# RWKV's gram matrices and state outputs: matmuls over 64 rows, two heads in turn, without zeros between them

## The chip, the cores and the metric

The kernel runs on one core of one Trainium2 chip. The time is the device time of one execution in microseconds (us), the median over runs. In the profile PE is TensorE's matmul, PEld its weight load, DVE VectorE, ACT ScalarE, POOL GpSimd, SP SyncE.

## The reference

One residual block of a decoder over 512 tokens of width 2048: an RWKV-7 time mixing and a sliding-window attention run in parallel, are merged by gates, and a gated ConvFFN follows. The change is inside the time mixing. Its recurrence has 16 heads of 64 channels:

```
def step(state, inp):
    r_t, k_t, v_t, w_t, ka_t, kb_t = inp        # ka = -kk, kb = kk * a
    sa = jnp.einsum('bhvk,bhk->bhv', state, ka_t)
    state = (state * w_t[:, :, None, :] + sa[..., None] * kb_t[:, :, None, :]
             + v_t[..., None] * k_t[:, :, None, :])
    y = jnp.einsum('bhvk,bhk->bhv', state, r_t)
    return state, y
_, y = lax.scan(step, state0, xs)
```

## The kernel before

The sequence is cut into 8 chunks (NCH) of 64 tokens (C), and the 16 heads into 8 pairs. A pair lies on the 128 partitions (rows): head 0 of the pair on rows 0 to 63, head 1 on rows 64 to 127 (`HV`). `early(p)` projects and prepares the inputs of pair p, `late(p, st)` does the recurrence by chunks, `final(p, st)` normalises and gates the result. Between the pairs `emit_gate` projects gate columns that are needed later. All projections go through `project` (L258 to L260), three float32r matmuls per weight tile into an accumulator `acc`; their weights are split into two parts by ACT (`whi`, L243) and DVE (`wlo`, L244).

In `late`, for every chunk n and head h:

- BKK holds the decayed kb and k of a head side by side as stationary operand (128 rows, 128 columns), BAR the decayed -kk and r as moving operand. The gram matmul (L645) gives all four products of a chunk for each head. Since both heads lie in the 128 rows of one matmul, BAR has a place for each head (`[P, NCH, 2, 2, C]`), in which the other head's rows are zero: 256 moving columns per chunk, half of them zeros in either half of the rows. Two chunks go to one PSUM bank of the pool `bulk`, which has three; DVE masks the bank into AB (L648) and MM (L649).
- AB is inverted in steps (X, AI, BT, BX; L650 to L710), with transposes through PE (L661, L671, L675, L707).
- The chain over the chunks: psG = AB and the state SV (L714), psU = BX and G (L718), psS = KK and UV (L725), and DVE makes the next state SV (L727).
- The output of a chunk: UV and MM (L735), to which the state SV and r of BAR are added (L737) in the same place of PSUM. Both have 128 rows and 64 stationary columns; SV has zeros in the rows of the other head's part of BAR or is met there by zeros.

All these are plain float32 matmuls, and one shows as two records on PE. The tiles and their dependencies are handled by a framework that also sets the order of each engine's instructions: unless the code pins it, it puts the program's instructions into an order of its own for each engine, so that projection matmuls stand between the steps of the chain.

Of the kernel before, what the change touches and what calls it, by code (L numbers as in the profile page):

```python
# [8 lines left out]
F32 = mybir.dt.float32  # L9
# [4 lines left out]
ALU = mybir.AluOpType  # L14
# [4 lines left out]
P = 128  # L19
# [3 lines left out]
C = 64  # L23
NCH = S // C
# [110 lines left out]
def block_kernel(ctx: ExitStack, tc: tile.TileContext, d: Dims, a: dict, out: bass.AP):  # L135
    nc = tc.nc
    act, dve, pool, pe, sync = nc.scalar, nc.vector, nc.gpsimd, nc.tensor, nc.sync
# [42 lines left out]
    def col(nm, i=0):  # L180
        return pcol[:, PR[nm] + i : PR[nm] + i + 1]
# [23 lines left out]
    def split(hi, lo, src, pin=free):  # L205
        pin(act.activation(hi, src, AF.Copy))
        pin(dve.tensor_tensor(lo, src, hi.bitcast(F32) if hi.dtype == F32R else hi, op=ALU.subtract))
# [75 lines left out]
    if True:  # L283
# [3 lines left out]
        with tc.tile_pool(name="x0_ps", bufs=6, space=PSUM) as ps0:  # L287
# [10 lines left out]
            for h in range(2):  # L298
                hs = slice(h * HT * P, (h + 1) * HT * P)
                for k in range(NK):  # L300
                    ps = ps0.tile([P, HT * P], F32, name="ps_x", tag="x")
                    for t in range(HT):
                        pe.transpose(ps[:, t * P : (t + 1) * P], xt[h * HT + t][:, k * P : (k + 1) * P], ident)
                    g = col("n1g", k)
# [43 lines left out]
        with ExitStack() as pt:  # L348
# [4 lines left out]
            def small():  # L353
                return mps.tile([P, S], F32, name="mi", tag="mi")
# [26 lines left out]
            for t in range(NKV):  # L381
# [12 lines left out]
                ps = small().rearrange("p (n c) -> p n c", c=P)  # L394
                for b in range(NT):
                    pe.transpose(ps[:, b], vf[:, b * P : (b + 1) * P], ident)
                ps = ps.rearrange("p n (h c) -> p n h c", c=HD)
# [16 lines left out]
            for g in range(NHK):  # L414
# [7 lines left out]
                for n in range(NT):  # L422
# [4 lines left out]
                    for j in range(GQ // 2):  # L427
                        for e in range(2):
                            hs = slice(e * HD, (e + 1) * HD)
# [4 lines left out]
                    for h in range(GQ):  # L434
                        slope = float(2.0 ** (-8.0 * (g * GQ + h + 1) / d.HQ))
                        dve.scalar_tensor_tensor(sc[:, h, k0:], K["dist"][:, k0:], slope, scp[h % 2][:, h // 2, k0:],
                                                 op0=ALU.mult, op1=ALU.add)
# [17 lines left out]
                    for kb in kbs:  # L455
                        ps = small().rearrange("p (h c) -> p h c", c=P)
# [3 lines left out]
                    ps = small()  # L460
                    for kb in kbs:
                        for i, (v, p) in enumerate(((0, 0), (0, 1), (1, 0))):
                            pe.matmul(ps, vhl[v][:, n - 1 + kb, g].rearrange("p e c -> p (e c)"),  # L463
                                      phl[p][:, kb].rearrange("p h c -> p (h c)"),
                                      start=kb == kbs[0] and i == 0, stop=kb == kbs[-1] and i == 2)
                    ps = ps.rearrange("p (h c) -> p h c", c=P)
# [6 lines left out]
        with ExitStack() as pr:  # L473
            lp = pr.enter_context(tc.tile_pool(name="lora", bufs=1, reuse_waits="tile"))
            zp_ = pr.enter_context(tc.tile_pool(name="zpad", bufs=1, reuse_waits="tile"))
            bd = pr.enter_context(tc.tile_pool(name="bd", bufs=1, reuse_waits="tile"))
# [15 lines left out]
            def wtile(tag, bufs=1):  # L492
                return wk.tile([P, S], F32, name=tag, tag=tag, bufs=bufs)

            def bulk():
                return blk.tile([P, S], F32, name="bulk", tag="bulk")
# [15 lines left out]
            for i in range(NG):  # L512
                acc = ztile(d.c_gd + i * P)
                t = wtile("lw")
# [11 lines left out]
            BV = bd.tile([P, NCH, P], F32, name="BV")  # L526
            pool.memset(BV, 0.0)
            BKK = bd.tile([P, NCH, P], F32, name="BKK")
            BAR = bd.tile([P, NCH, 2, 2, C], F32, name="BAR")
            pool.memset(BAR[0:C, :, 1], 0.0)  # L530
            pool.memset(BAR[C:P, :, 0], 0.0)
            AB, MM, KK, SV, UV = (bd.tile([P, NCH, 2, C], F32, name=n) for n in ("AB", "MM", "KK", "SV", "UV"))
            pool.memset(SV[0:C, 0, 0], 0.0)
            pool.memset(SV[C:P, 0, 1], 0.0)
# [4 lines left out]
            def r3(ap, c=C):  # L539
                return ap.rearrange("p (n c) -> p n c", c=c)  # L540

            HV = ((0, C), (C, P))
# [72 lines left out]
            def late(p, st):  # L615
                ag, Ei, kk, kb, k2, rz, vz, bon = st
                Eex, Ein = Et[:, :, 0:C], Et[:, :, 1:]
                kb3, k23, Ei3, kk3, rz3, vz3 = (r3(x) for x in (kb, k2, Ei, kk, rz, vz))
                for h, (lo, hi) in enumerate(HV):
                    ol, oh = HV[1 - h]  # L620
                    hs = slice(lo, hi)
                    dve.tensor_tensor(BKK[hs, :, lo:hi], kb3[hs], Ei3[hs], op=ALU.mult)
                    dve.tensor_tensor(BKK[hs, :, ol:oh], k23[hs], Ei3[hs], op=ALU.mult)
                    dve.scalar_tensor_tensor(BAR[hs, :, h, 0], kk3[hs], -1.0, Eex[hs], op0=ALU.mult, op1=ALU.mult)
                    dve.tensor_tensor(BAR[hs, :, h, 1], rz3[hs], Ein[hs], op=ALU.mult)
                    act.activation(BV[hs, :, ol:oh], vz3[hs], AF.Copy)
                ee = wk.tile([P, NCH], F32, name="ee", tag="ee")
                act.activation(ee, Et[:, :, C], AF.Copy)

# [4 lines left out]
                HN = NCH // 2  # L634

                def mb(nm, n, h=None):
                    m = K[nm] if h is None else K[nm][h[0] : h[1]]
                    return m.unsqueeze(1).to_broadcast([m.shape[0], n, m.shape[-1]])

                BKE = wk.tile([P, NCH, P], F32, name="BKE", tag="BKE")  # L640
                dve.tensor_tensor(BKE, BKK, ee.unsqueeze(2).to_broadcast([P, NCH, P]), op=ALU.mult)
                for n0 in range(0, NCH, 2):
                    ps = bulk().rearrange("p (q c) -> p q c", c=P)
                    for j in range(2):
                        pe.matmul(ps[:, 2 * j : 2 * j + 2].rearrange("p q c -> p (q c)"), BKK[:, n0 + j],  # L645
                                  BAR[:, n0 + j].rearrange("p h a c -> p (h a c)"), start=True, stop=True)
                    q2 = lambda t: t[:, n0 : n0 + 2].rearrange("p n h c -> p (n h) c")
                    dve.tensor_tensor(q2(AB), ps[:, :, 0:C], mb("strict", 4), op=ALU.mult)  # L648
                    dve.tensor_tensor(q2(MM), ps[:, :, C:P], mb("incl", 4), op=ALU.mult)  # L649
                for g in range(2):  # L650
                    ns = slice(g * HN, (g + 1) * HN)
                    for h, (lo, hi) in enumerate(HV):
                        own = AB[lo:hi, ns, h]
                        (dve.tensor_copy if h else act.copy)(BX[lo:hi, ns, lo:hi], own)
                        dve.tensor_tensor(tt[lo:hi, ns], own, mb("m1", HN, (lo, hi)), op=ALU.mult)
                        act.copy(own, BAR[lo:hi, ns, h, 0])
                    dve.tensor_tensor(tt[:, ns], tt[:, ns], mb("istack", HN), op=ALU.add)
                    split(X[:, 0, ns], X[:, 1, ns], tt[:, ns])
                    ps = bulk().rearrange("p (n c) -> p n c", c=P)
                    for j in range(HN):  # L660
                        pe.transpose(ps[:, j], BX[:, g * HN + j], ident)  # L661
                    at_ = wk.tile([P, HN, P], F32, name="at_", tag="at_")
                    dve.scalar_tensor_tensor(at_, ps, SG, mb("idsg", HN), op0=ALU.mult, op1=ALU.add)
                    split(AI[:, 0, ns], AI[:, 1, ns], at_)
                    for i in range(2):
                        dve.tensor_tensor(BT[:, i, ns], AI[:, i, ns], mb("t1bd", HN), op=ALU.mult)
                for g in range(2):
                    ns = slice(g * HN, (g + 1) * HN)
                    ps = bulk().rearrange("p (n c) -> p n c", c=P)
# [3 lines left out]
                    ps = bulk().rearrange("p (n h c) -> p n h c", h=2, c=C)  # L673
# [14 lines left out]
                for m in LEVELS[1:]:  # L688
                    last = m == LEVELS[-1]
                    ps = bulk()  # L690
# [4 lines left out]
                    ps = bulk()  # L695
# [4 lines left out]
                    if not last:  # L700
                        act.activation(X[:, 0], r3(ps), AF.Copy, scale=sc)
                        dve.scalar_tensor_tensor(X[:, 1], r3(ps), sc, X[:, 0], op0=ALU.mult, op1=ALU.subtract)
                        for g in range(2):
                            ns = slice(g * HN, (g + 1) * HN)
                            ps = bulk().rearrange("p (n c) -> p n c", c=P)
# [5 lines left out]
                for n in range(NCH):  # L711
                    ps = chn.tile([P, C], F32, name="psG", tag="chn")
# [4 lines left out]
                    ps = chn.tile([P, C], F32, name="psU", tag="chn")  # L717
# [5 lines left out]
                    ps = chn.tile([P, C], F32, name="psS", tag="chn")  # L723
                    for h, (lo, hi) in enumerate(HV):
                        pe.matmul(ps[lo:hi], KK[:, n, h], UV[:, n, h], start=True, stop=True)  # L725
                    for h, (lo, hi) in enumerate(HV):
                        dve.scalar_tensor_tensor(SV[lo:hi, n + 1, h], SV[lo:hi, n, h], ee[lo:hi, n : n + 1], ps[lo:hi],  # L727
                                                 op0=ALU.mult, op1=ALU.add)


                ps = bulk()
                for n in range(NCH):
                    for h, (lo, hi) in enumerate(HV):
                        dst = r3(ps)[lo:hi, n]
                        pe.matmul(dst, UV[:, n, h], MM[:, n, h], start=True, stop=n == 0)  # L735
                        if n:
                            pe.matmul(dst, SV[:, n, h], BAR[:, n, h, 1], start=False, stop=True)  # L737
                yhl = wk.tile([P, 2, S], F32R, name="yhl", tag="rhl")
                split(yhl[:, 0], yhl[:, 1], ps)
                return ag, bon, yhl  # L740
# [23 lines left out]
            for p in range(NP):  # L764
                lt = late(p, st)
                if p + 1 < NP:
                    st = early(p + 1)
                final(p, lt)
                for _ in range(GATES_PER_PAIR * NK // 16):
                    emit_gate()  # L770
# [72 lines left out]
    with ExitStack() as pbb:  # L843
# [8 lines left out]
        g = {}  # L852
        for m, i in order:
            hi, lo, r0, n, gi = parts[i]
# [11 lines left out]
            if second:  # L866
                w = min(XC, d.D)
                for e in range(m * XC, (m + 1) * XC, w):
                    t, c0 = divmod(e, d.D)
# [475 lines left out]
def build(nc, arrays, d):  # L1345
    aps = {
        k: nc.dram_tensor(f"in_{k}_dram", v.shape, mybir.dt.from_np(v.dtype), kind="ExternalInput").ap()
        for k, v in arrays.items()
    }
    out = nc.dram_tensor("out_0_dram", (S, d.D), F32, kind="ExternalOutput").ap()  # L1350
    with tile.TileContext(nc) as tc:
        block_kernel(tc, d, aps, out)
# [11 lines left out]
```

## Time and profile before

| | |
|---|---|
| median of 3 runs | 2932.01 us (2930.34 to 2932.07) |
| the profiled execution | 2934.35 us, span 2932.5 us |
| granted TensorE clock | 0.997 |
| the eight pairs, 330 to 1190 us of the span | PE 856 us busy of 860 |
| gram matmuls L645 | 64, two records each |
| output matmuls L735, L737 | 128 and 112, two records each |

In the timeline a row is a run of equal instructions: the start in us from the span's start, the length in us, engine, line, operation, the tile written and the tiles read, then for PE the shape of the stationary operand as rows*columns and of the moving one as rows x elements, and the count. A bracket behind it is idle time before it and what ended that. The ends of matmuls are modelled and successive matmuls overlap, so the distance between starts says how long one occupies PE.

### The profile page before, as it was taken

Reading aid. Unit: us, or ns where it says so; the run is one execution under the profiler, and the core shown is the slowest. Engines: PE = TensorE matmul, PEld = TensorE weight load, DVE = VectorE, ACT = ScalarE, POOL = GpSimd, SP = SyncE. Lnnn points to the kernel's source line nnn. Section 1 sums busy time; section 2 is a strip of 40 time slices with the busy share of each in tenths; the row PEclk is TensorE's granted clock in tenths of the full one; section 3 lists DMA queues with packets and bytes.
Section 4 is the critical chain, followed back from the end, with each engine's and each line's share of the span. In section 5 each row is a group of like instructions: output and inputs, shape, how many; then the busy total and the mean of one; then the engine's idle time right before and its main releaser. Section 6 shows DMA issues by size and latency. Waiting matters only on the chain.

```text
span 2932.5 us, 47976 instructions
## 1 busy us (share of the span) xinstructions
PE 2885.5 (98%) x18654; PEld 2457.4 (84%) x18654; DVE 1978.9 (67%) x3279; ACT 1322.7 (45%) x2147; POOL 219.3 (7%) x286
## 2 busy tenths in 40 slices
PE   7999999999999999999999899999999999999999
PEld 5777777777777777788888899999999999888887
DVE  4577666766766766445567877777777777665555
ACT  4345434434434434332356455455555554544444
POOL 0001000000000000101000001101111011000000
PEclk9999999999999999999999999999999999999999
DMA  7855755656655655877877789888888888877775
GB/s 212 221 151 160 184 136 147 167 137 150 166 137 151 165 134 149 264 226 231 294 248 237 191 232 240 237 226 225 230 238 241 233 226 231 313 240 244 255 258 188
DMA packets 225140, 609.44 MB, mean 208 GB/s; under 512 B 24768, under 2 KB 44944, under 8 KB 223888
## 3 DMA queue, kind: packets, MB, share of 16 engines
q1 hardware_dynamic: 157504, 434.92, 45.1%
q0 software_dynamic: 36064, 132.14, 23.5%
q10 hardware_dynamic: 31344, 39.31, 3.9%
q8 instruction: 146, 2.39, 0.3%
q14 instruction: 82, 0.67, 0.1%
HBM read 556.62 MB, written 174.43 MB: 249 GB/s over the span
## 4 chain that ended last, share of the span: by engine, by line
PE 92%; DMA 3%; DVE 2%; ACT 2%; issue 1%; ACTq 0%; SPq 0%; POOL 0%; DVEq 0%; POOLq 0%
PE X L1065 17%; PE acc L260 11%; PE acc L259 11%; PE acc L258 10%; PE X L932 10%; PE Y L932 8%; PE Y L1065 8%; PE Z L1065 4%; PE bulk L645 1%; PE bulk L707 1%; PE psG L714 1%; PE psS L725 1%; PE mi L463 1%; PE scp L430 1%; PE bulk L553 1%; PE bulk L684 1%
## 5 line engine op out<-in xcount | busy, mean ns | idle before, releaser
L260 PE MATMUL acc<-xhi,wlo 128*128 128x512 f32 x1152 | 471.4, 409 | 0.0
L258 PE MATMUL acc<-xhi,whi 128*128 128x512 f32 x1152 | 465.4, 404 | 3.2 <-DVE xlo L306 1.9
L259 PE MATMUL acc<-xlo,whi 128*128 128x512 f32 x1152 | 465.3, 404 | 0.0
L243 ACT ACTIVATE whi<-raw 128x512 fp32r<-128x512 f32 x352 | 220.1, 629 | 440.9 <-PE acc L259 345.8
L925 DVE TENSOR_TENSOR wlo<-raw,whi 128x1024 fp32r<-128x1024 f32 x210 | 257.1, 1225 | 206.1 <-ACT whi L924 206.0
L244 DVE TENSOR_TENSOR wlo<-raw,whi 128x512 fp32r<-128x512 f32 x352 | 240.5, 689 | 213.0 <-ACT whi L243 206.7
L924 ACT ACTIVATE whi<-raw 128x1024 fp32r<-128x1024 f32 x210 | 222.6, 1060 | 289.3 <-PE X L932 150.9
L1065 PE MATMUL X<-b,whi 128*128 128x256 f32 x1472 | 270.6, 284 | 2.3 <-DVE u L1085 0.9
L1065 PE MATMUL X<-t,whi 128*128 128x256 f32 x1408 | 260.0, 285 | 10.0 <-DVE u L1085 9.5
L1048 DVE TENSOR_TENSOR wlo<-raw,whi 128x1024 fp32r<-128x1024 f32 x176 | 215.1, 1223 | 78.3 <-ACT whi L1047 78.1
L1065 PE MATMUL Y<-t,whi 128*128 128x256 f32 x1408 | 257.1, 283 | 0.0
L258 PEld LDWEIGHTS acc<-xhi,whi 128*128 128x128 f32 x1152 | 217.5, 189 | 44.0 <-issue 3.2
L260 PEld LDWEIGHTS acc<-xhi,wlo 128*128 128x128 f32 x1152 | 217.1, 189 | 43.5 <-issue 2.5
L259 PEld LDWEIGHTS acc<-xlo,whi 128*128 128x128 f32 x1152 | 217.4, 189 | 42.6 <-issue 2.7
L1047 ACT ACTIVATE whi<-a 128x1024 fp32r<-128x1024 f32 x132 | 139.3, 1056 | 215.2 <-DVE a L1041 213.8
L1065 PEld LDWEIGHTS X<-b,whi 128*128 128x128 f32 x1472 | 230.8, 193 | 3.1 <-issue 2.4
L1065 PEld LDWEIGHTS X<-t,whi 128*128 128x128 f32 x1408 | 221.9, 194 | 10.6 <-DVE u L1085 6.9
L1065 PEld LDWEIGHTS Y<-t,whi 128*128 128x128 f32 x1408 | 219.6, 192 | 0.0
L1065 PE MATMUL X<-b,wlo 128*128 128x256 f32 x736 | 209.2, 284 | 2.1 <-DVE wlo L1048 2.1
L1048 DVE TENSOR_TENSOR wlo<-a,whi 128x1024 fp32r<-128x1024 f32 x132 | 161.7, 1226 | 67.3 <-ACT whi L1047 66.7
L1065 PE MATMUL X<-t,wlo 128*128 128x256 f32 x704 | 200.4, 285 | 0.0
L1065 PE MATMUL Y<-t,wlo 128*128 128x256 f32 x704 | 199.2, 283 | 0.0
(343 smaller groups left out, 6073.1 us busy)
## 6 DMA issues: line engine op xcount, KB each, us to landing
raw<-in_w_up_dram SPq DMA_DIRECT2D x180, 512.0 KB
raw<-in_w_z_dram SPq DMA_DIRECT2D x288, 256.0 KB
s_dn<-in_w_dn_dram POOLq DMA_DIRECT2D x88, 512.0 KB, 6.5
raw<-in_w_up_dram POOLq DMA_DIRECT2D x88, 512.0 KB, 8.4
raw<-s_dn SPq DMA_DIRECT2D x88, 512.0 KB
raw<-in_w_dn_dram SPq DMA_DIRECT2D x66, 512.0 KB
a<-in_w_up_dram SPq DMA_DIRECT2D x48, 512.0 KB
s_dn<-in_w_dn_dram SPq DMA_DIRECT2D x44, 512.0 KB
```

The source lines that it names most:

```text
L243: act.activation(hi, raw, AF.Copy)
L244: dve.tensor_tensor(lo, raw, hi.bitcast(F32), op=ALU.subtract)
L258: pe.matmul(acc, whi[:, j], xhi[:, k], start=first, stop=False)
L259: pe.matmul(acc, whi[:, j], xlo[:, k], start=False, stop=False)
L260: pe.matmul(acc, wlo[:, j], xhi[:, k], start=False, stop=last)
L430: pe.matmul(scp[e][:, j, k0:], qn[j][hs, ts], kd[g][hs, n * P - BLK + k0 : (n + 1) * P], start=True, stop=True)
L924: act.activation(whi, wr, AF.Copy)
L925: dve.tensor_tensor(wlo, wr, whi.bitcast(F32), op=ALU.subtract)
L932: pe.matmul(dst, l[:, q, ts], r[:, es], start=fst and j == 0, stop=lst and j == 2, skip_group_check=True)
L1047: pin(act.activation(hi, t, AF.Copy))
L1048: pin(dve.tensor_tensor(lo, t, hi.bitcast(F32), op=ALU.subtract))
L1065: pin(pe.matmul(ps, l[:, k], r[:, k], start=start and k + i == 0, stop=last and i == 2, skip_group_check=True))
```

## The change

BAR loses the zeros: it is `[P, NCH, 2, C]`, with -kk and r of both heads each in its own half of the rows. The DVE writes of BAR run over 128 partitions, two per pair instead of four. The gram matmuls become two per chunk, one over rows 0 to 63 and one over rows 64 to 127, with 128 moving columns each; the two heads go into two banks, four chunks per bank. The masks then work by head on four chunks instead of by two chunks of both heads. The second output matmul (L738 now) takes only the head's 64 rows of SV and BAR.

```
-            BAR = bd.tile([P, NCH, 2, 2, C], F32, name="BAR")
-            pool.memset(BAR[0:C, :, 1], 0.0)
-            pool.memset(BAR[C:P, :, 0], 0.0)
+            BAR = bd.tile([P, NCH, 2, C], F32, name="BAR")
...
-                    dve.scalar_tensor_tensor(BAR[hs, :, h, 0], kk3[hs], -1.0, Eex[hs], op0=ALU.mult, op1=ALU.mult)
-                    dve.tensor_tensor(BAR[hs, :, h, 1], rz3[hs], Ein[hs], op=ALU.mult)
                     act.activation(BV[hs, :, ol:oh], vz3[hs], AF.Copy)
+                dve.scalar_tensor_tensor(BAR[:, :, 0], kk3, -1.0, Eex, op0=ALU.mult, op1=ALU.mult)
+                dve.tensor_tensor(BAR[:, :, 1], rz3, Ein, op=ALU.mult)
...
-                for n0 in range(0, NCH, 2):
-                    ps = bulk().rearrange("p (q c) -> p q c", c=P)
-                    for j in range(2):
-                        pe.matmul(ps[:, 2 * j : 2 * j + 2].rearrange("p q c -> p (q c)"), BKK[:, n0 + j],
-                                  BAR[:, n0 + j].rearrange("p h a c -> p (h a c)"), start=True, stop=True)
-                    q2 = lambda t: t[:, n0 : n0 + 2].rearrange("p n h c -> p (n h) c")
-                    dve.tensor_tensor(q2(AB), ps[:, :, 0:C], mb("strict", 4), op=ALU.mult)
-                    dve.tensor_tensor(q2(MM), ps[:, :, C:P], mb("incl", 4), op=ALU.mult)
+                for g in range(2):
+                    ns = slice(g * HN, (g + 1) * HN)
+
+                    pss = [bulk().rearrange("p (q c) -> p q c", c=P) for _ in HV]
+                    for j in range(HN):
+                        for ps, (lo, hi) in zip(pss, HV):
+                            n = g * HN + j
+                            pe.matmul(ps[:, j], BKK[lo:hi, n], BAR[lo:hi, n].rearrange("p a c -> p (a c)"), start=True, stop=True)
+                    for h, ps in enumerate(pss):
+                        dve.tensor_tensor(AB[:, ns, h], ps[:, :, 0:C], mb("strict", HN), op=ALU.mult)
+                        dve.tensor_tensor(MM[:, ns, h], ps[:, :, C:P], mb("incl", HN), op=ALU.mult)
...
-                        act.copy(own, BAR[lo:hi, ns, h, 0])
+                        act.copy(own, BAR[lo:hi, ns, 0])
...
-                            pe.matmul(dst, SV[:, n, h], BAR[:, n, h, 1], start=False, stop=True)
+                            pe.matmul(dst, SV[lo:hi, n, h], BAR[lo:hi, n, 1], start=False, stop=True)
```

The framework orders the engines anew. On PE, at the gram of the second pair (pair 1), the rows stood like this before (line, operation, tile written and tiles read, size of the output, count):

```order
L260 MATMUL acc<-xhi,wlo 128x512
L645 MATMUL bulk<-BAR,BKK 128x256 x8
L258 MATMUL acc<-xhi,whi 128x512
L259 MATMUL acc<-xlo,whi 128x512
L260 MATMUL acc<-xhi,wlo 128x512
L258 MATMUL acc<-xhi,whi 128x512
L259 MATMUL acc<-xlo,whi 128x512
L260 MATMUL acc<-xhi,wlo 128x512
L661 MATMUL bulk<-ident,BX 128x128 x4
```

Six projection matmuls stood between the gram and the first transposes of BX. On PE at the same place after the change:

```order
L260 MATMUL acc<-xhi,wlo 128x512
L647 MATMUL bulk<-BAR,BKK 128x128 x16
L258 MATMUL acc<-xhi,whi 128x512
L259 MATMUL acc<-xlo,whi 128x512
L260 MATMUL acc<-xhi,wlo 128x512
L258 MATMUL acc<-xhi,whi 128x512
L259 MATMUL acc<-xlo,whi 128x512
L260 MATMUL acc<-xhi,wlo 128x512
L258 MATMUL acc<-xhi,whi 128x512
L259 MATMUL acc<-xlo,whi 128x512
L260 MATMUL acc<-xhi,wlo 128x512
L662 MATMUL bulk<-ident,BX 128x128 x4
```

Nine stand there now, and the eight gram matmuls are sixteen. Within the sixteen, with the numbers of the banks (4431 and 4445 are head 0's two banks, 4432 and 4446 head 1's) and with what an instruction waits for, the rows on PE from the fourth chunk on are:

```order
L647 MATMUL bulk_4431<-BAR_2919,BKK_2918 128x128
L647 MATMUL bulk_4432<-BAR_2919,BKK_2918 128x128
L647 MATMUL bulk_4445<-BAR_2919,BKK_2918 128x128 x4
L647 MATMUL bulk_4446<-BAR_2919,BKK_2918 128x128 [waits DVE_49,PE_49]
L647 MATMUL bulk_4446<-BAR_2919,BKK_2918 128x128 x3
L258 MATMUL acc_5016<-xhi_187,whi_5019 128x512 [waits Activation_49]
```

The first four chunks go head by head in turn; of the last four, head 0's stand together, and then head 1's, the first of which waits for DVE. The other pairs but pair 0 have the same order.

On PE, at two steps of the chain in the output of a chunk, before (psS belongs to the chain, the bulk rows are the output):

```order
L336 MATMUL bulk<-ident,rq_5096 8x128
L725 MATMUL psS<-UV,KK 64x64
L735 MATMUL bulk<-MM,UV 64x64
L737 MATMUL bulk<-BAR,SV 64x64
L725 MATMUL psS<-UV,KK 64x64
L735 MATMUL bulk<-MM,UV 64x64
L737 MATMUL bulk<-BAR,SV 64x64
L577 MATMUL bulk<-wl,thw 128x128 x2
```

And the same place on PE after the change, where lines have moved by one or two:

```order
L336 MATMUL bulk<-ident,rq_5106 8x128
L575 MATMUL bulk<-wl,thw 128x128
L726 MATMUL psS<-UV,KK 64x64
L736 MATMUL bulk<-MM,UV 64x64
L738 MATMUL bulk<-BAR,SV 64x64
L575 MATMUL bulk<-wl,thw 128x128
L726 MATMUL psS<-UV,KK 64x64
L736 MATMUL bulk<-MM,UV 64x64
L738 MATMUL bulk<-BAR,SV 64x64
L575 MATMUL bulk<-wl,thw 128x128 x2
```

The output matmuls keep their places behind the chain's; a projection-like matmul has moved in between the two heads. In the whole program L738 stands 112 times directly behind L736 or L726, both of 128 rows and 64 columns; behind it stands a matmul of 128 columns 94 times and one of 128 rows and 64 columns 18 times.

## The prediction

> **What bounds the kernel now.** I read the page first: busy time and the chain that ended last.
>
> ```profile
> span 2932.5 us, 47976 instructions
> PE 2885.5 (98%) x18654; PEld 2457.4 (84%) x18654; DVE 1978.9 (67%) x3279; ACT 1322.7 (45%) x2147; POOL 219.3 (7%) x286
> PE 92%; DMA 3%; DVE 2%; ACT 2%; issue 1%; ACTq 0%; SPq 0%; POOL 0%; DVEq 0%; POOLq 0%
> ```
>
> TensorE is busy 98% of the span and carries 92% of the last chain. Next came the table by stages, for the stretch in which the eight pairs of heads are worked on:
>
> ```profile
> 330.00:1190.00 860.00, 856.01 (x6143) 645.68 (x6142) 572.94 (x1255) 351.31 (x708) 53.77 (x68) 1.00 0.58 149
> ```
>
> PE is busy 856.01 of 860 us there, at full clock, and DVE 572.94. Between the small matmuls of a pair stand projection matmuls (acc), so nearly every wait of the chain is already filled. What the change adds to PE lengthens the kernel one to one, and what it takes from DVE or POOL is worth nothing unless PE waits for it. The answer for the tile BAR lists what the change touches:
>
> ```profile
> L737 PE MATMUL bulk<-BAR,SV x224: 222/222/222, 391.6 to 1183.9; 128*64 128x64 f32 x112
> L645 PE MATMUL bulk<-BAR,BKK x128: 377/379/483, 335.7 to 1111.9; 128*128 128x256 f32 x128
> L625 DVE TENSOR_TENSOR BAR<-rz,Et x16: 676/687/691, 331.3 to 1086.4; 64x512 f32<-64x512 f32 x16
> ```
>
> One f32 matmul is two records on PE: 64 gram matmuls give 128, 112 output matmuls 224. The durations (222, 379 ns) overlap, so I price by the distance from start to start, in the timeline.
>
> **The output matmuls.** These are consecutive rows of PE's timeline (start, length, line, shape, count), one step of the chain in pair 0:
>
> ```profile
> 390.73 0.40 PE L259 MATMUL acc<-xlo,whi 128*128 128x512 f32 x1
> 390.96 0.40 PE L260 MATMUL acc<-xhi,wlo 128*128 128x512 f32 x1
> 391.29 0.33 PE L725 MATMUL psS<-UV,KK 128*64 128x64 f32 x2
> 391.45 0.28 PE L735 MATMUL bulk<-MM,UV 128*64 128x64 f32 x2
> 391.57 0.28 PE L737 MATMUL bulk<-BAR,SV 128*64 128x64 f32 x2
> 391.78 0.50 PE L258 MATMUL acc<-xhi,whi 128*128 128x512 f32 x1
> 392.12 0.40 PE L259 MATMUL acc<-xlo,whi 128*128 128x512 f32 x1
> ```
>
> A projection matmul takes 0.23 us (390.73 to 390.96), a pair of 128x64 records 0.12 us (391.45 to 391.57). Where the stationary tile changes shape, from 128*128 to 128*64, there is more: 390.96 to 391.29 is 0.33, so 0.10 over, and the pair behind it takes 0.16 instead of 0.12. I read this as PE emptying the array (0.10) and then loading weights with nothing running over the load (0.04). Going back: L737 to L258 is 0.21, 0.09 over, and L258 to L259 is 0.34, 0.11 over.
>
> After the change the second output matmul uses 64 rows: its shape is 64*64, while the one ahead of it (L735, now L736) stays 128*64. L737 had its neighbour's shape and cost 0.12; L738 is a third shape. In the new order all 112 L738 stand directly behind a 128*64 matmul. Behind them come 94 times a 128*128 matmul (a change of shape there before as well, at the same price) and 18 times another 128*64 one, a further new change. That makes 130 new changes. Streaming itself gets no shorter: 64 moving columns either way.
>
> The trace has no change from 128*64 to 64*64. Nearest is one where rows alone change, 128*128 to 64*128, in the attention scores (L430), which work on 64 rows with the two heads in turn:
>
> ```profile
> 191.68 0.39 PE L259 MATMUL acc<-xlo,whi 128*128 128x512 f32 x1
> 192.00 0.49 PE L430 MATMUL scp<-kd,qn 64*128 64x128 f32 x4
> 192.42 0.50 PE L260 MATMUL acc<-xhi,wlo 128*128 128x512 f32 x1
> 192.76 0.39 PE L258 MATMUL acc<-xhi,whi 128*128 128x512 f32 x1
> ...
> 131.39 0.39 PE L260 MATMUL acc<-xhi,wlo 128*128 128x512 f32 x1
> 131.71 0.72 PE L430 MATMUL scp<-kd,qn 64*128 64x128 f32 x8
> 132.35 0.50 PE L258 MATMUL acc<-xhi,whi 128*128 128x512 f32 x1
> 132.69 0.39 PE L259 MATMUL acc<-xlo,whi 128*128 128x512 f32 x1
> ```
>
> 191.68 to 192.00 is 0.32, again 0.09 over. Columns alone (L260 to L725) and rows alone cost the same, so I take the cost of entering a 64-column shape, 0.10 + 0.04 = 0.14 us: 130 x 0.14 = 18.2 us, all on PE and uncovered. The ends: nothing (0), if rows may change freely between shapes of 64 columns; 0.09 + 0.11 = 0.20 as for 128 columns, 130 x 0.20 = 26 us. A gain is excluded, since no streaming is saved.
>
> The Trainium skill (TensorEngine Tiling (Array Packing), Key Properties) says that changing the tiling mode, unlike moving between tiles of one mode, drains TensorE, with no figure; by it the sum keeps the 18.2 and the end of 0 falls away. No run here shows it yet for these two shapes.
>
> **The gram matrices.** Before, eight matmuls stand in a row in pair 1:
>
> ```profile
> 446.98 0.39 PE L260 MATMUL acc<-xhi,wlo 128*128 128x512 f32 x1
> 447.21 3.62 PE L645 MATMUL bulk<-BAR,BKK 128*128 128x256 f32 x16
> 450.47 0.58 PE L258 MATMUL acc<-xhi,whi 128*128 128x512 f32 x1
> 450.89 0.39 PE L259 MATMUL acc<-xlo,whi 128*128 128x512 f32 x1
> ```
>
> From 447.21 to 450.89, less one projection slot of 0.23, is 3.45 us. After, they are 16 matmuls of shape 64*128 moving 128 columns, exactly L430's shape at 192.00 and 131.71. With 4 records (two in each half of the rows) the block lasts 0.42 to the next start, with 8 (four in each) 0.64: so 0.11 per record of one half, the other half running beside it at no cost. Around it stand 0.10 on entry and 0.11 on the matmul behind. A block with m records in the longer half costs 0.10 + 0.42 + 0.11 (m - 2) + 0.11. Fully alternating, m = 16: 2.17 us, a gain of 1.28.
>
> The order on PE does not alternate fully. It has the first eight in turn (8 records in each half), then four of head 0 in a row, then four of head 1 behind a wait for DVE; those last two stretches run one behind the other. So m = 8 + 8 + 8 = 24: 0.63 + 22 x 0.11 = 3.05 us. The wait is for head 0's first bank, which two mask products must have read:
>
> ```profile
> 447.84 0.69 DVE L244 TENSOR_TENSOR wlo<-raw,whi 128x512 fp32r<-128x512 f32 x1 [2.02 <-ACT whi L243]
> 448.45 0.42 DVE L648 TENSOR_TENSOR AB<-bulk,cst 128x256 f32<-128x256 f32 x1
> 448.79 0.41 DVE L649 TENSOR_TENSOR MM<-bulk,cst 128x256 f32<-128x256 f32 x1
> 449.13 0.42 DVE L648 TENSOR_TENSOR AB<-bulk,cst 128x256 f32<-128x256 f32 x1
> ```
>
> DVE is free at 448.45; the first eight end at about 447.21 + 0.10 + 0.21 + 7 x 0.11 = 448.29. A record lasts some 0.17 beyond its slot (L645: 379 ns against 0.21 from start to start), so I let head 0's masks begin at 448.55 and end near 449.3 (0.34 to the second, which lasts 0.41). PE reaches head 1 at 448.29 + 0.88 = 449.17 and waits 0.15. The gain is 3.45 - 3.05 - 0.15 = 0.25 us, 7 x 0.25 = 1.8 us.
>
> Pair 0 is ordered otherwise. There PE waited for DVE before:
>
> ```profile
> 335.74 1.89 PE L645 MATMUL bulk<-BAR,BKK 128*128 128x256 f32 x8
> 337.28 0.58 PE L258 MATMUL acc<-xhi,whi 128*128 128x512 f32 x1
> 337.70 0.40 PE L259 MATMUL acc<-xlo,whi 128*128 128x512 f32 x1
> 339.20 1.99 PE L645 MATMUL bulk<-BAR,BKK 128*128 128x256 f32 x8 [1.10 <-DVE bon L612]
> 340.84 0.58 PE L260 MATMUL acc<-xhi,wlo 128*128 128x512 f32 x1
> ```
>
> DVE now writes BAR in two operations over 128 partitions instead of four over 64 (687 ns each), so it is about 1.4 us earlier, and the 1.10 goes: 1.1 us gained. I count nothing for the rest of that gram, which is split in two blocks with waits of its own. In the other pairs PE doesn't wait for the writes of BAR, and the same saving is worth nothing. The masks keep count and size; BKK, the copies and the transposes stay; two POOL memsets at 274 us go, off the path. The transposes of BX stand nine projection matmuls behind the gram instead of six, 9 x 0.23 = 2.1 us, about what the masks that now end last need.
>
> **Sum.** 18.2 - 1.8 - 1.1 = +15.3 us. The profiled execution took 2934.35 us around a span of 2932.5 and becomes 2949.7; the median of the runs, 2932.01, lies 2.3 lower and becomes **2947 us**, 0.5% slower.
>
> **Rivals.** (a) *The change of rows is free* while the columns stay 64: then only the 2.9 us gained at the gram remain, 2929, not slower. For it: the row halves share columns. Against it: 0.09 us at 192.00, where only rows change. It decides for no loss once a change of shape costs under 2.9/130 = 0.02 us. (b) *Half the price:* the emptying is paid on entering 64*64 alone and no load is laid bare, 112 x 0.10 = 11.2, less 2.9, is +8.3: 2940. (c) *The gram overlaps fully*, m = 16: 7 x 1.28, and in pair 0 two blocks of m = 8 (1.29 each) for two of 1.73 (335.74 to 337.70 less 0.23), 0.9; 9.8 gained and 18.2 - 9.8 = +8.4: 2940. The rows of L430 show the overlap, the written order speaks against it. The Trainium skill (TensorE: Matmul & The Clock Gate, Part 3) has matmuls in distinct row groups run concurrently, which is what L430 shows and what (c) would need throughout. (d) *Dearer:* masks that come behind one more wlo (L244, 0.6 us up to the next start) in seven pairs, 4 us: 2951; or 0.20 per change, 26 - 2.9 = +23: 2955.
>
> **How the numbers follow.** The forecast with its own range 2942 to 2951 gets 0.62; (a) 0.08, (b) 0.10, (c) 0.05, (d) 0.12, and 0.03 for (a) and (c) together, 2922. The range 2938 to 2955 holds the forecast, (b), (c) and (d). A measurement can tell about 0.2%, 5.9 us: slower 0.88 (forecast, b, c, d), same 0.08 (a), faster 0.04.
>
> **What would show it.** In PE's timeline after: L736 to L738 about 0.21 to 0.22 apart instead of 0.12 (right), or still 0.12 (rival a). The L738 pair to a projection matmul 0.25 instead of 0.21, as its own first load is bare. The gram of pair 1 from its first start to the matmul behind it about 3.1 us long, with a short wait for DVE MM (L650) before head 1's last four. A pair some 2 us longer (130/8 x 0.14 less 0.25). I am wrong if the 18 changes back, or the drains, run beside other work, or if PE waits for BX longer than it did.

## The result, and the profile after

| | median us | lowest to highest | runs |
|---|---|---|---|
| before | 2932.01 | 2930.34 to 2935.64 | 5 |
| after | 2947.66 | 2941.75 to 2952.69 | 5 |

The ratio is 1.0052, with a 95% interval of 1.0040 to 1.0063: the changed kernel is 0.5% slower. 2947 us, and 2938 to 2955, were predicted. The profiled execution of after is its longest run: 2952.69 us around a span of 2950.9, at a mean granted clock of 0.997.

The page of after, span, busy time and the chain that ended last:

```profile
span 2950.9 us, 48234 instructions
PE 2903.3 (98%) x18782; PEld 2464.2 (84%) x18782; DVE 1973.5 (67%) x3263; ACT 1323.1 (45%) x2147; POOL 216.8 (7%) x284
PE 93%; DMA 2%; DVE 2%; ACT 1%; issue 1%; ACTq 0%; DVEq 0%; POOLq 0%; SPq 0%
```

PE has 17.8 us more of busy time than before (2903.3 against 2885.5), and the span 18.4 us more. DVE has 5.4 us less and POOL 2.5, and neither shows in the time. The same stretch of the pairs as before, in the table by stages:

```profile
330.00:1190.00 860.00, 857.33 (x6176) 641.79 (x6174) 560.78 (x1218) 348.06 (x698) 52.78 (x67) 1.00 0.60 146
```

PE is as full as it was (857.33 of 860 us, at full clock), so PE doesn't wait more than it did: it takes longer for the same work. How much longer is read from the start of a pair's gram to the start of the next one's. PE's timeline of before has at the last pair (pair 7):

```profile
1108.45 0.39 PE L260 MATMUL acc<-xhi,wlo 128*128 128x512 f32 x1
1108.68 0.59 PE L645 MATMUL bulk<-BAR,BKK 128*128 128x256 f32 x2
```

and that of after has there:

```profile
1121.59 0.39 PE L260 MATMUL acc<-xhi,wlo 128*128 128x512 f32 x1
1121.91 0.60 PE L647 MATMUL bulk<-BAR,BKK 64*128 64x128 f32 x6
```

Pair 1 starts at 447.21 before and at 448.55 after (below). Six periods are 661.47 us before and 673.36 after, so one is 110.25 and 112.23 us: **+1.98 us for each pair**. This period is the measure that the experiments go by. It moved much less than the time in the one repetition there is: in a second profiled execution of after it was 112.28, while the spans were 2950.9 and 2946.7.

The output of a chunk in PE's timeline of after, at the place that the prediction shows of before:

```profile
390.79 0.50 PE L258 MATMUL acc<-xhi,whi 128*128 128x512 f32 x1
391.12 0.40 PE L259 MATMUL acc<-xlo,whi 128*128 128x512 f32 x1
391.45 0.33 PE L726 MATMUL psS<-UV,KK 128*64 128x64 f32 x2
391.61 0.28 PE L736 MATMUL bulk<-MM,UV 128*64 128x64 f32 x2
391.82 0.33 PE L738 MATMUL bulk<-BAR,SV 64*64 64x64 f32 x2
392.08 0.50 PE L260 MATMUL acc<-xhi,wlo 128*128 128x512 f32 x1
```

L736 to L738 is 0.21 us (0.12 before), and L738 to the projection matmul 0.26 (0.21 before): 0.09 + 0.05 = 0.14 us for entering the shape 64*64. The records themselves got longer by this too, not shorter for their half of the rows; the answer for the tile BAR says so for all 224 (222 ns before):

```profile
L738 PE MATMUL bulk<-BAR,SV x224: 218/242/267, 390.5 to 1200.9; 64*64 64x64 f32 x112
```

The gram of pair 1, on PE:

```profile
448.24 0.39 PE L260 MATMUL acc<-xhi,wlo 128*128 128x512 f32 x1
448.55 3.22 PE L647 MATMUL bulk<-BAR,BKK 64*128 64x128 f32 x32
451.70 0.50 PE L258 MATMUL acc<-xhi,whi 128*128 128x512 f32 x1
452.04 0.40 PE L259 MATMUL acc<-xlo,whi 128*128 128x512 f32 x1
```

From 448.24 to 452.04, less two slots of 0.23, is 3.34 us, against 3.45 before. The masks on DVE at that time:

```profile
449.10 0.69 DVE L244 TENSOR_TENSOR wlo<-raw,whi 128x512 fp32r<-128x512 f32 x1 [2.02 <-ACT whi L243]
449.75 0.42 DVE L649 TENSOR_TENSOR AB<-bulk,cst 128x256 f32<-128x256 f32 x1
450.09 0.41 DVE L650 TENSOR_TENSOR MM<-bulk,cst 128x256 f32<-128x256 f32 x1
```

And two rows of the answer for the tile BAR, on what its readers and writers waited for, and who waited for them (us in all, times):

```profile
its engine sat idle before it (us, times) until:
...
  PE bulk L647: 1.5, 7
who waited for it (us, times):
...
  PEld bulk L647: 1.5, 7
```

PE's weight load (PEld) sits idle once in each of seven pairs, 1.5 us in all, 0.21 each, ahead of head 1's last four. The order printed above the prediction lists two waits there, for DVE and for PE itself (`[waits DVE_49,PE_49]`). Head 0's MM ends on DVE at 450.50, and the load starts at 450.62. The profile names PE's own gram matmul as what ended the wait, not the masks. The two came so close together that the run can't tell them apart; if the profile names the right one, earlier masks alone would have gained nothing.

Last, PE's waits in the pairs 1 to 7. Before, first a row of the list of waits (total, times, longest), then its instance in pair 1 in the timeline:

```profile
PE bulk L684 <- ACT AI L206: 1.5, 6, 0.3
```

```profile
459.07 0.20 PE L684 MATMUL bulk<-XIW,AI 128*128 128x64 f16 x1 [0.26 <-ACT AI L206]
```

After, the same list has only this:

```profile
PE bulk L336 <- DVE rq L197: 0.4, 1, 0.4
```

A pair has two AI tiles, one for each half of its chunks, and the triangular inverse begins with matmuls on them. Before, the first matmul on the second AI waited 0.25 us in each pair for ACT to write it. After, it stands here:

```profile
460.57 0.40 PE L258 MATMUL acc<-xhi,whi 128*128 128x512 f32 x1
460.81 0.20 PE L685 MATMUL bulk<-XIW,AI 128*128 128x64 f16 x1
```

In the new order 22 projection matmuls stand between the gram and it instead of 19, two of them directly ahead of it, and the wait is gone. The prediction has no term for it.

### The profile page after: what moved, and what is told of

Same layout as the page of the kernel before. It is cut to its first block, busy times and chain, and to the rows that moved or that the text cites. A ratio compares the mean times of both kernels' runs of the same rounds, so it can differ in the third digit from the quotient of the medians.

```text
span 2950.9 us, 48234 instructions
## 1 busy us (share of the span) xinstructions
PE 2903.3 (98%) x18782; PEld 2464.2 (84%) x18782; DVE 1973.5 (67%) x3263; ACT 1323.1 (45%) x2147; POOL 216.8 (7%) x284
## 3 DMA queue, kind: packets, MB, share of 16 engines
q8 instruction: 147, 2.41, 0.3%
## 4 chain that ended last, share of the span: by engine, by line
PE 93%; DMA 2%; DVE 2%; ACT 1%; issue 1%; ACTq 0%; DVEq 0%; POOLq 0%; SPq 0%
PE X L1066 17%; PE acc L260 11%; PE acc L259 11%; PE acc L258 11%; PE X L933 10%; PE Y L933 8%; PE Y L1066 8%; PE Z L1066 4%; PE bulk L738 1%; PE bulk L708 1%; PE psS L726 1%; PE psG L715 1%; PE bulk L647 1%; PE mi L463 1%; PE scp L430 1%; PE bulk L685 1%
## 5 line engine op out<-in xcount | busy, mean ns | idle before, releaser
L258 PE MATMUL acc<-xhi,whi 128*128 128x512 f32 x1152 | 463.6, 402 | 4.7 <-ACT whi L243 2.8
L1049 DVE TENSOR_TENSOR wlo<-raw,whi 128x1024 fp32r<-128x1024 f32 x176 | 214.9, 1222 | 77.8 <-ACT whi L1048 77.8
L258 PEld LDWEIGHTS acc<-xhi,whi 128*128 128x128 f32 x1152 | 217.3, 189 | 48.0 <-ACT whi L243 4.0
```

The costliest lines, as they stand in the source:

```text
L258: pe.matmul(acc, whi[:, j], xhi[:, k], start=first, stop=False)
L1049: pin(dve.tensor_tensor(lo, t, hi.bitcast(F32), op=ALU.subtract))
```

## The experiments

Theory A is the prediction's: the loss is PE's price for each change of shape in the order in which its matmuls are issued, 0.14 us into 64 columns, so it follows the number of changes and not the number of 64-row matmuls. The rivals put the loss elsewhere: in the gram and the order that comes with it, or in the 64-row output matmul itself, wherever it stands. The texts ahead of each run use letters for them and give each one's numbers. Each run is compared with the kernel before on the same chip.

**The outputs alone.** The kernel before, with its zeros, gram and masks, and only the second output matmul on 64 rows:

```
-pe.matmul(dst, SV[:, n, h], BAR[:, n, h, 1], start=False, stop=True)
+pe.matmul(dst, SV[lo:hi, n, h], BAR[lo:hi, n, h, 1], start=False, stop=True)
```

> Only the output matmul is changed (64 rows of SV and of BAR's own half); the gram matrices, the zeros in BAR and the masks stay as before. Theory A (the time goes into changes of the stationary shape on PE, each 0.09 us of emptying and 0.05 us of bare weight load): its order has 112 changes into 64*64 and 19 more out of it into 128*64, 131 x 0.14 = 18.3 us, so about 2950 us, slower than the whole change. Rival B (the time goes into the gram part: single-head stretches, the wait for the masks, the transposes behind them): 2932 us, as before.

It took 2952.94 us against 2933.11, ratio 1.0075 (1.0061 to 1.0088), +19.8 us. A period is 112.65 us, +2.41. In PE's timeline, at the place shown above:

```profile
391.32 0.28 PE L735 MATMUL bulk<-MM,UV 128*64 128x64 f32 x2
391.53 0.33 PE L737 MATMUL bulk<-BAR,SV 64*64 64x64 f32 x2
391.78 0.50 PE L258 MATMUL acc<-xhi,whi 128*128 128x512 f32 x1
```

The distances are those of after, 0.21 and 0.25. This one edit, which only takes half the rows from 112 matmuls, carries more than the whole loss. PE's order has 633 changes of shape instead of 502; the 131 more at 0.14 are 18.3 us, or 2.29 a pair.

**The gram alone.** The change's gram and masks on the kernel before, with `BAR[lo:hi, n, h]` out of the BAR with zeros, and outputs over 128 rows:

> Only the gram matmuls and their masks are changed (64 rows, two heads, two banks); BAR keeps its zeros and its four writes, the output matmuls stay at 128 rows. Theory A: the gram of a pair gains 0.1 us in seven pairs, a little more in pair 0, so 2930 to 2932 us. Rival B: about 2947 us, all of the loss.

2933.16 us, ratio 1.0002 (0.9994 to 1.0011). Rival B falls: none of the loss is here. The period is 109.83, -0.41 us, about what the profile of after says: 0.11 in the gram, and the 0.25 of the wait for AI, which this run's list of waits no longer has. The time doesn't show it, and pair 0 gained nothing, though a little more was expected there. In this profiled execution the granted TensorE clock reads 0.63 from 336 to 342 us and 0.85 from there to 350, just in pair 0's gram, where it was 1.00 in before and in after; pair 1 starts 1.0 us later than before (448.25 against 447.21). Why the clock fell there stays open.

The two parts add in the period: +2.41 and -0.41 make +2.00, against the +1.98 of the whole change.

**The outputs of a pair in one block.** The whole change, with the 14 output matmuls L738 of a pair behind the chain, head 0's seven and then head 1's (`pin` keeps a matmul directly behind the one written ahead of it; the start and stop flags follow the new order):

```
-pe.matmul(dst, UV[:, n, h], MM[:, n, h], start=True, stop=n == 0)
-if n:
-    pe.matmul(dst, SV[lo:hi, n, h], BAR[lo:hi, n, 1], start=False, stop=True)
+pe.matmul(r3(ps)[lo:hi, n], UV[:, n, h], MM[:, n, h], start=n == 0, stop=False)
...
+for h, (lo, hi) in enumerate(HV):
+    for n in range(1, NCH):
+        pin(pe.matmul(r3(ps)[lo:hi, n], SV[lo:hi, n, h], BAR[lo:hi, n, 1], start=False, stop=n == NCH - 1))
```

> The whole change, but the 14 output matmuls over 64 rows of a pair stand in one block behind the last one over 128 rows, head 0's seven and then head 1's. The count and size of the matmuls are those of the whole change; the changes into and out of 64*64 fall from 130 extra to 8, while the order has 11 more changes into 128*64 and back. Theory A: 2947.7 - 122 x 0.14 + 11 x 0.35 = 2934 to 2935 us. Rival C (a 64-row matmul of this form is itself dearer, for instance because it accumulates on the matmul before it over another shape): stays near 2947 us.

2939.94 us, ratio 1.0024 (1.0015 to 1.0033). The same 112 matmuls of 64 rows, over half of the loss gone: the price is on the change of shape, not on the matmul. The block in PE's timeline:

```profile
530.79 0.33 PE L735 MATMUL bulk<-MM,UV 128*64 128x64 f32 x2
531.04 1.66 PE L738 MATMUL bulk<-BAR,SV 64*64 64x64 f32 x28
532.64 0.51 PE L260 MATMUL acc<-xhi,wlo 128*128 128x512 f32 x1
```

14 matmuls take 1.60 us, 0.11 each: one head behind the other, with hardly any overlap. But the time is some 5 us over what theory A expected. The period is +0.69 us. Two things were missing in that expectation. All kinds of changes of shape counted in PE's order are 502 before, 514 with the gram alone and 551 here, since the matmuls that fill the chain are placed otherwise too: 37 more than with the gram alone, at 0.14 each 0.65 us a pair. And a new wait stands in this run's list:

```profile
PE bulk L336 <- DVE rq L197: 1.2, 6, 0.2
```

0.65 + 0.20 less the 0.41 of the gram is +0.44, against +0.69. The last 0.25 us a pair stays open.

**The heads in turn within the block.** The two loops of the block above change places, so that a head's matmul is followed by the other head's:

> As the run with the output in one block, but the 14 matmuls of the block take the two heads in turn. The changes of shape are the same. If matmuls in different rows and columns of the array run side by side although they write one bank, the block lasts 0.8 us instead of 1.6, 8 x 0.8 = 6.5 us less: 2933 us against 2940. If they don't (one bank), 2940.

2934.99 us, ratio 1.0007 (0.9998 to 1.0015).

```profile
530.75 1.03 PE L738 MATMUL bulk<-BAR,SV 64*64 64x64 f32 x28
531.72 0.50 PE L260 MATMUL acc<-xhi,wlo 128*128 128x512 f32 x1
```

The same 28 records take 0.97 us instead of 1.60: the two heads run side by side, 0.14 for two matmuls instead of 0.23. Only the order in which they are issued differs. The 0.63 us are in the period (110.26, 0.68 under the block by heads). The time fell less than the 6.5 us expected: 6.8 us over before for the block by heads, 3.2 here.

**The gram strictly in turn.** The kernel before with the 64-row gram, in which the second four chunks alternate too, starting with head 1:

```
+for g in range(2):
...
+    for j in range(HN):
+        for h in ((0, 1), (1, 0))[g]:
...
+            mm = pe.matmul(pss[h][:, j], BKK[lo:hi, n], BAR[lo:hi, n, h].rearrange("p a c -> p (a c)"), start=True, stop=True)
+            if j or h != g:
+                pin(mm)
```

> Only the gram part is changed, as in the run with the gram alone, but the matmuls of the two heads are kept strictly in turn on PE, so that the second four chunks overlap as the first four do and projection matmuls can stand ahead of them while the masks are awaited. Theory A (what ate the gram's gain was the order head 0, then head 1, and the wait): per pair a block of 10 and one of 8 records in the longer half, 1.51 + 1.29 = 2.80 us instead of 3.45, 0.65 x 8 = 5 us gained, about 2927 us. Rival D (a 64-row gram gains nothing because weight loads, not the moving columns, set its pace): 2932 us or more.

2930.91 us, ratio 0.9990 (0.9981 to 0.9999); the period is 109.40, -0.85 us.

```profile
446.28 0.39 PE L260 MATMUL acc<-xhi,wlo 128*128 128x512 f32 x1
446.60 1.39 PE L650 MATMUL bulk<-BAR,BKK 64*128 64x128 f32 x18
447.91 0.50 PE L258 MATMUL acc<-xhi,whi 128*128 128x512 f32 x1
448.25 0.39 PE L259 MATMUL acc<-xlo,whi 128*128 128x512 f32 x1
448.48 0.40 PE L260 MATMUL acc<-xhi,wlo 128*128 128x512 f32 x1
448.80 1.16 PE L650 MATMUL bulk<-BAR,BKK 64*128 64x128 f32 x14
450.00 0.30 PE L667 MATMUL bulk<-ident,BX 128*128 128x128 f32 x1
```

446.28 to 448.25 less two slots, and 448.48 to 450.00 less one, are 1.51 and 1.29: 2.80 us (2.91 with the bare load of the transpose behind it, if that is the 0.11 of other changes) against 3.45 before and 3.34 in after. That is about the 0.65 expected, and the wait for AI, gone here as well, makes it about 0.9, against 0.85 measured. The block of 2.80 us answers rival D: in turn, the 64-row gram does gain. The time gained less (2.2 us) than seven or eight such periods and missed the 2927 expected. In the profiled execution the clock was low in pair 0 here as well (0.72 from 336 to 342 us), and PE waited 2.96 us for a weight part (whi) at 1222 us.

**The outputs by two.** The first experiment's outputs, but the two heads' 64-row matmuls of a chunk directly behind one another:

```
 for h, (lo, hi) in enumerate(HV):
...
+    pe.matmul(r3(ps)[lo:hi, n], UV[:, n, h], MM[:, n, h], start=True, stop=n == 0)
+for h, (lo, hi) in enumerate(HV):
     if n:
+        pin(pe.matmul(r3(ps)[lo:hi, n], SV[lo:hi, n, h], BAR[lo:hi, n, h, 1], start=False, stop=True))
```

> As the run with the output alone (gram, masks and zeros as before, 112 output matmuls over 64 rows), but the two heads' 64-row matmuls of a chunk stand directly behind one another, so that the changes into 64*64 are halved from 112 to 56 and none leads from there to 128*64. By kinds against before: 9 fewer into 128*64 from 128 columns, 64 fewer back, 56 into 64*64 (0.14 each), 56 back (0.20): -1.3 - 12.8 + 7.8 + 11.2 = +5 us. Theory A: about 2938 us, a quarter of the loss of the run with the output alone; if the two heads, which lie in different rows and columns, also run side by side, 56 x 0.12 = 6.5 us less, 2931 to 2932. Rival C (each 64-row matmul is dearer by itself): 112 as before, about 2951 us.

2933.12 us against 2931.75, ratio 1.0004 (0.9996 to 1.0013): the 19.8 us of the first experiment are gone.

```profile
392.54 0.28 PE L734 MATMUL bulk<-MM,UV 128*64 128x64 f32 x2
392.75 0.33 PE L737 MATMUL bulk<-BAR,SV 64*64 64x64 f32 x4
393.01 0.50 PE L260 MATMUL acc<-xhi,wlo 128*128 128x512 f32 x1
```

Entry (0.21) and exit (0.26) are those of after, but four records lie between them instead of two, in the same 0.26 us. Half the changes into 64*64 are gone (56 instead of 112), and of each two matmuls one is covered by the other. In numbers of a pair: 39 changes more than before in all, 0.68 us, less seven covered matmuls of 0.12, 0.84, is -0.16, against -0.10 measured (110.14).

**Both turns together.** After, with the gram in turn and the block with the heads in turn:

> The whole change with both orders mended: gram matmuls of the two heads strictly in turn, and the 64-row output matmuls of a pair in one block, heads in turn. The gram in turn gives 0.85 us a pair (profile of the run with it alone), the block costs 0.7 us a pair in the run with it and loses up to 0.8 of that where the heads overlap. Theory A with overlap: 2925 to 2928 us, faster than before; without overlap: 2932 to 2934.

2930.16 us, ratio 1.0001 (0.9991 to 1.0010), over the 2925 to 2928 expected with overlap; the period is 109.90, -0.35. By its parts, the block in turn (+0.01) and what the gram in turn gains over the plain one (0.85 - 0.41), -0.43 was to come. The block's new wait for rq is in this run's list as well (1.0 us in six).

**The changed kernel once more,** on the chip on which the heads in turn, the outputs by two and both turns ran:

> The whole change once more, beside the others on one chip: 2947 to 2950 us. If the parts add, it lies at the run with the output alone plus the run with the gram alone less what pair 0 gains by two fewer writes of BAR (about 1 us).

2950.41 us against 2931.75, ratio 1.0068 (1.0056 to 1.0081), the period 112.28. The loss stands in the same place; the time of one kernel, though, went from 2944.29 to 2959.08.

**The best order found.** After, with the gram in turn and the outputs by two:

> Both parts of the change with the two orders that cost least so far: gram matmuls strictly in turn (period of a pair 109.35 us in its profile, against 110.20 before), and the two heads' 64-row output matmuls directly behind one another per chunk (110.10). Theory A: they add to a period of 109.2 to 109.3, 8 x 0.9 to 1.0 = 7 to 8 us less than before, 2924 to 2926 us, faster by 0.25%. If, as in the run with both parts and one output block per pair (109.90), half a microsecond a pair comes back through the order of the rest, 2929 to 2930 us, the same as before.

2928.89 us against 2932.52, ratio 0.9985 (0.9976 to 0.9994): 0.15% faster than before, the lowest median of the study, and by the ratios to before 0.7 to 0.8% faster than the changed kernel. The period is 109.27, -0.97, as the gram in turn (-0.85) and the outputs by two (-0.10) give together. The time expected was lower by 3 us or more. In the output projection, after the pairs, the first matmul into its tile Y comes 6.6 us earlier than before (1448.39 against 1454.97), the end of the span 5.4 us. Where the rest goes: between the last gram and that matmul stand PE's waits for loaded weights, and they differ from run to run. That stretch took 346.3 us before, 348.3 here, 350.7 in after and 347.4 in the repetition of after (some 2 us of the last two are the changes of shape of the last pair). The row of L258 on the page of after has part of it; its last column is PE's idle time there, 2.8 us of it behind whi, while the repetition has none such:

```profile
L258 PE MATMUL acc<-xhi,whi 128*128 128x512 f32 x1152 | 463.6, 402 | 4.7 <-ACT whi L243 2.8
```

```profile
L258 PE MATMUL acc<-xhi,whi 128*128 128x512 f32 x1152 | 463.1, 402 | 1.9 <-DVE xlo L306 1.9
```

So a gain of a few us in the pairs shows in the period and is blurred in the time.

The periods side by side, in us against before (110.25). The terms are read from the rows and runs above, so the table shows whether they add, not whether they were foreseen:

| kernel | by the sum of its terms | measured |
|---|---|---|
| after | 130/8 x 0.14 - 0.11 - 0.18 = +1.99 | +1.98 |
| outputs alone | 131/8 x 0.14 = +2.29 | +2.41 |
| gram alone | - 0.11 - 0.25 = -0.36 | -0.41 |
| gram in turn | - 0.65 - 0.25 = -0.90 | -0.85 |
| outputs by two | +0.68 - 0.84 = -0.16 | -0.10 |
| block, by heads | +0.65 + 0.20 - 0.41 = +0.44 | +0.69 |
| block, in turn | +0.44 - 0.63 = -0.19 | +0.01 |
| gram in turn, outputs by two | - 0.85 - 0.10 = -0.95 | -0.97 |

The 0.18 of after is the wait for AI (0.25) less the 0.4 us in six pairs that the wait for rq takes. All changes of shape are priced at 0.14. With the 0.20 that a change back to 128 columns costs, the sums of outputs by two and of the block by heads become -0.23 and +0.52, so they are no better than some 0.15 us a pair.

## Why the prediction was right

**The output matmuls, 18.2 us: confirmed.** 0.09 on entry and 0.05 behind it stand at each of them, as was read from other changes of shape in the trace of before. The outputs alone cost 19.8 us, or 0.15 for each of 131 changes. That no gain comes of half the rows was right too; streaming is 64 columns either way. The Trainium skill (TensorEngine Tiling (Array Packing), Key Properties) has a drain at each change of tiling mode; the trace agrees, 0.09 us here, and here only the rows change.

**The gram, 1.8 us: right in mechanism, too large.** 0.11 us a pair came instead of 0.25. Two terms were off. The wait ahead of head 1's last four was 0.21 instead of 0.15, and the profile puts its end down to PE's own matmul, where the prediction waited for the masks alone. And the block without it took 3.34 - 0.21 = 3.13 us instead of 3.05: the first of head 1's four, behind the wait, takes 0.18 us to the next start instead of 0.11, as its weight load is covered by nothing. The four of one head and then the four of the other did run one behind the other, as the order said, and the gram in turn shows what that costs: about half a us.

**Pair 0, 1.1 us: near in sum by luck (0.9 came), wrong in its step.** With two writes of BAR less, DVE was to be 1.4 us earlier and the wait of 1.10 to go. In after PE's timeline has:

```profile
335.58 1.16 PE L647 MATMUL bulk<-BAR,BKK 64*128 64x128 f32 x16
336.67 0.49 PE L258 MATMUL acc<-xhi,whi 128*128 128x512 f32 x1
337.82 1.88 PE L647 MATMUL bulk<-BAR,BKK 64*128 64x128 f32 x16 [0.66 <-DVE bon L610]
339.63 0.50 PE L259 MATMUL acc<-xlo,whi 128*128 128x512 f32 x1
339.98 0.60 PE L662 MATMUL bulk<-ident,BX 128*128 128x128 f32 x4
```

0.66 us of it is still there. The first row here is DVE's bon before, which released PE, the second is the same after:

```profile
338.47 0.68 DVE L612 TENSOR_TENSOR bon<-vz,bulk 128x512 f32<-128x512 f32 x1
337.08 0.69 DVE L610 TENSOR_TENSOR bon<-vz,bulk 128x512 f32<-128x512 f32 x1
```

DVE did come 1.4 us earlier, as was said. But PE is there 0.94 us earlier too (idle from 337.16 instead of 338.10): the gram's first block takes 1.09 us to the next start instead of 1.54, and one projection matmul stands behind it instead of two. The prediction held PE's side fixed. From the gram's start to the first transpose of BX, less the projection matmuls between, it is 3.95 us (339.98 - 335.58 - 0.45), against 4.84 before (335.74 to 342.63, with nine of them, 2.05). So 0.9 us were gained, 0.44 from the wait and the rest in the gram's first block, for which nothing was counted.

**Not in the sum: the wait for AI.** 0.25 us a pair went with the new order, in which more projection matmuls stand ahead of the second AI's first matmul; the gram alone, which has the same order there, is without the wait too, and the outputs alone keep it. The transposes of BX don't wait, as was said. Seven such waits are 1.8 us, less the 0.4 of the new wait for rq; that is as much as the gram's shortfall (1.0 us) and a little more, so the period came out at +1.98 where 2.0 was said. That the sum is this close is luck in part: two misses cancel. So is the median, 0.7 us from the forecast: the same kernel once more was 18.7 us over before, where +15.3 was said.

**The rivals.** (a), a free change of rows, falls by the 0.21 between L736 and L738, and so does (b), half the price, by the 0.26 behind L738 and the 19.8 us of the outputs alone. (c), full overlap in the gram, didn't happen in the written order, and the gram in turn shows what it would have been worth. Of (d), no further wlo stands ahead of the masks (the one at 449.10, ahead of head 0's AB at 449.75, has its like at 447.84 before), and 0.20 per change did not show. Two small slips of the sums change nothing here: (c) leaves out the 1.1 us of pair 0, and the chances named for slower add up to 0.89, not 0.88. The profiled execution's 2952.7 us lie 3 over the forecast for it, in the stage behind the pairs.

## What to carry to other kernels

A matmul over fewer rows was no cheaper by itself on this bound TensorE: count the changes of shape in the order in which PE issues its matmuls, and price each by the distance of starts at a change that the trace already shows. Halves of the rows paid here where matmuls of the two halves stood directly behind one another, in turn; written by half, they ran one after the other. Where a list of waits names small waits that come back in each round, look at what the new order puts ahead of them: here that was as large as the gram's term. And where a wait is to go because its releaser comes earlier, ask whether the engine that waits comes earlier too.

## What the runs showed of the hardware

Matmuls of shape 64*64 of two heads, in different rows and different columns, ran side by side while writing into one PSUM bank in different partitions: 28 records in 0.97 us in turn, 1.60 us by heads. The Trainium skill (TensorEngine Tiling (Array Packing), Restrictions and Gotchas) says that different row tiles cannot access the same PSUM bank at the same time; here, where the columns differ as well, the 0.97 us show no such delay. A change of rows alone (128*64 to 64*64, 0.09 us and a bare load of 0.05) costs as much as the change from 128*128 to 128*64 (0.10 and 0.04).
